# Memory values of layers two to four as Strassen's seven block products, in a one-core decoder trunk

## The chip, the cores and the metric

One core of a Trainium2 chip runs the whole kernel, in one launch. The metric is device time in microseconds from start to end of one execution; the median of three runs before the change is 2577.76 us. The engines are TensorE (PE in the profile, with its weight loads as PEld), VectorE (DVE), ScalarE (ACT), GpSimd (POOL) and SyncE (SP, which issues the weight loads).

## The reference

Four decoder layers over 256 tokens of width 2048. Each layer has self attention of one of three kinds, and four memory heads of size 256 that attend to 256 memory tokens. All four layers read the same normalized memory, each with its own weights:

```python
mem_n = _rmsnorm(mem, mem_norm)                 # (1, 256, 2048)
for i in range(DEPTH):                          # 4 layers
    h = _rmsnorm(x, norm_in[i])
    ...                                         # self attention, memory queries mq, gate
    mem_out = _memory_attention(mq, mem_n @ w_mem_kv[i])   # keys: columns 0..1023, values: 1024..2047
    y = jnp.concatenate([self_out, mem_out], axis=-1) * jax.nn.silu(gate)
    x = x + y @ w_out[i]
return _rmsnorm(x, final_norm)
```

The change concerns the second half of the columns of `mem_n @ w_mem_kv[i]`, the values, for i = 1, 2, 3. Everything is float32.

## The kernel before, in words

Products are made in float32r with each operand split in a high part and a low part, and three of the four partial products are kept. `split` (lines 60 and 69) makes the parts: ScalarE copies the source to the high part (`wh` from `wr`), VectorE subtracts it from the source for the low part (`wl`). Weights come by `stage`: SP loads 512 KB, four row blocks of 256 columns or two of 512, in a `wr` tile, of which there are five; `wh` and `wl` have three buffers each.

`memory()` runs ahead of the layers. It keeps the memory's features in `mT`, four tiles of four blocks of 128 features, high and low, 256 tokens. For each layer `i` and each half `p_` it does one values group and two keys groups:

- values: `rows_by(mT, 16, w, 0, (MEMW + p_ * 512, 512), "mv")`. For each of 16 feature blocks and each of two blocks of 128 tokens, three matmuls (lines 265 to 267) with the features as stationary weights and 512 weight columns streaming. `values()` scales the rows by `mrstd`, splits them and has GpSimd's queue store them (line 409).
- keys: `columns_by` (lines 285 and 289), twice with 256 columns, with the weights stationary and the features streaming, 512 wide for high and low features together and 256 wide for the low weights. `keys()` sums the two halves (`total`, line 296), multiplies by the token scales `mbc` (line 416), splits and has GpSimd's queue store them (line 418).

Each `stage` calls `other_work()`, which takes two steps of a queue of small jobs; `nm.first_chunk` (weighted parts of the first layer's input, line 198, and its square sums) is put there from the second half on. The layers then fetch keys and values back with GpSimd's queue. The instructions of an engine run in the order that a scheduler gave them when the program was built; GpSimd does almost no arithmetic: small copies that hold back table DMAs (`tick`, line 149), clearing, and eight casts of 128x256 (`xl`, line 827) in the sparse layer's selection. Behind the outputs of a layer, line 1146 adds a PSUM result to the residual `x`.

Of the kernel before, what the change touches and what calls it, by code (L numbers as in the profile page):

```python
# [2 lines left out]

# [28 lines left out]
def kernel(ctx: ExitStack, tc: tile.TileContext, a: dict, out: bass.AP,  # L32
# [10 lines left out]
    def misc(name, dt=F32):  # L43
        return ps.tile([P, 512], dt, name=name, tag="mp", bufs=4)

    def tmp(name, n=512, dt=F32):
        return wk.tile([P, n], dt, name=name, tag=f"t{n}", bufs=3)
# [5 lines left out]
    def f32(ap):  # L53
        return ap.bitcast(F32)

    def part_tile(dt=F32R):
        return wk.tile([P, 512], dt, name="hl", tag="hl", bufs=2)

    def copy_act(o, i, scale=1.0):
        inst = nc.scalar.activation(o, i, AF.Copy, scale=scale)  # L60
        if pinned:
            tc.keep_in_program_order(inst)
# [4 lines left out]
    def split(hi, lo, src):  # L67
        copy_act(hi, src)
        nc.vector.tensor_sub(lo, src, f32(hi))  # L69
# [58 lines left out]
    def bias_table(v):  # L128
        oh = wk.tile([32, N_TAB], F32, name="oh", tag="t512", bufs=3)
        tc.keep_in_program_order(nc.gpsimd.dma_start(oh, a["c_onehot"]))  # L130
        rb = wk.tile([32, 32], F32, name="rb", tag="rb", bufs=1)
        tc.keep_in_program_order(nc.gpsimd.dma_start(rb, a["rel_bias"]))
        mk = wk.tile([32, N_TAB], F32, name=f"mk{v}", tag="t512", bufs=3)
        tc.keep_in_program_order(nc.gpsimd.dma_start(mk, a["c_tabmask"][v]))
        pt = misc("pt")
        nc.tensor.matmul(pt[:32, :N_TAB], rb, oh, start=True, stop=True)
        tb = act.tile([P, 2, 4, S], F32, name=f"tb{v}", tag="y", bufs=2)[:32, 0, :2, :].rearrange(
            "p a b -> p (a b)")[:, :N_TAB]
        nc.vector.tensor_add(tb, pt[:32, :N_TAB], mk)
        nc.gpsimd.dma_start(flat[v], tb)  # L140
# [65 lines left out]
    def stage(w, k0, m, cols, each=None):  # L206

        n = cols[1] if len(cols) == 2 else cols[1] * cols[4]
        wr = wp.tile([P, ST * 512], F32, name="wr", tag="wr", bufs=WR)
        src = w[k0 * P:(k0 + m) * P, :].rearrange("(k p) n -> p k n", p=P)  # L210
        dst = wr[:, :m * n].rearrange("p (k n) -> p k n", k=m)
        if each is not None:
            for k in range(m):
                tc.keep_in_program_order(nc.sync.dma_start(dst[:, k, :], src[:, k, cols[0]:cols[0] + n]))
                each(k0 + k)
        elif len(cols) == 2:
            nc.sync.dma_start(dst, src[:, :, cols[0]:cols[0] + n])
        else:
            c0, r, step, off, width = cols
            for k in range(m):  # L220
                nc.sync.dma_start(dst[:, k, :].rearrange("p (r c) -> p r c", r=r),
                                  src[:, k, c0:c0 + r * step].rearrange("p (r c) -> p r c", r=r)
                                  [:, :, off:off + width])
        return wr, n
# [4 lines left out]
    def other_work():  # L229
        for _ in range(2):  # L230
            if steps and next(steps[0], None) is None:
                steps.pop(0)
# [34 lines left out]
                    nc.tensor.matmul(acc[t][:, :n], xl, wh[:, :n], start=False, stop=last)  # L267
        return acc

    def columns_by(xt, kts, w, k0, cols, name):  # L270

        acc = [ps.tile([P, 2, S], F32, name=f"acc_{name}{j}", tag="acc", bufs=4) for j in range(2)]
        for s in range(0, kts, 2 * ST):
            m = min(2 * ST, kts - s)
            wr, n = stage(w, k0 + s, m, cols)
            other_work()
            for k2 in range(0, m, 2):
                wh, wl = parts_of(wr, k2 * S, 2 * S)
                for k in range(2):
                    kt = s + k2 + k  # L280
                    q = xt[kt // 4]

                    for j in range(2):
                        o = k * S + j * P
                        nc.tensor.matmul(acc[j], wh[:, o:o + P], q[:, :, kt % 4, :],  # L285
                                         start=kt == 0, stop=False)
                    for j in range(2):
                        o = k * S + j * P
                        nc.tensor.matmul(acc[j][:, 0, :], wl[:, o:o + P], q[:, 0, kt % 4, :],  # L289
                                         start=False, stop=kt == kts - 1)  # L290
        return acc
# [73 lines left out]
    def memory():  # L365
        mrstd = cst.tile([P, 2], F32, name="mrstd")
        m16 = cst.tile([P, 2], F32, name="m16")
        mbc = act.tile([P, S], F32, name="mbc", tag="kr", bufs=1)
        mT = [act.tile([P, 2, 4, S], F32R, name="mT", tag=f"big{c}") for c in range(4)]
        mss = small("mss", 8, bufs=2)  # L370

        def each(k):

            if k % 2 and k < 15:
                mft[(k + 1) // 4].load((k + 1) // 2 % 2)
            if k == 15:
                tc.keep_in_program_order(nc.sync.dma_start(ident, a["c_ident"]))
                nc.vector.tensor_copy(identr, ident)

        def prepare(k):  # L380
            c = k // 4
            weighted_parts(mT[c], mft[c].q, k % 4, c * 4)

        def memory_rows(c):
            q = act.tile([P, 2, 512], F32, name="mrow", tag="pq", bufs=PQ)
            for t in range(2):
                tc.keep_in_program_order(
                    nc.sync.dma_start(q[:, t, :], min_[t][:, c * 512:(c + 1) * 512]))
            return q

        def row_scales(mrow):
            for c in range(4):
                for t in range(2):
                    square_sum(mss[:, t * 4 + c:t * 4 + c + 1], mrow[c][:, t, :])
            s2 = small("ms2", 2)
            nc.vector.tensor_reduce(s2, mss.rearrange("p (t c) -> p t c", t=2), AX.X, OP.add)
            rsqrt_mean(mrstd, s2, D)
            nc.vector.tensor_scalar(m16, mrstd, 0.0625, None, op0=OP.mult)
            spread(mbc, m16)

        def values(i, p_, acc):
            v = [act.tile([P, 2, 512], F32R, name="mv", tag="aux", bufs=AUX) for z in range(2)]
            for t in range(2):
                sc = mrstd[:, t:t + 1]
                copy_act(v[0][:, t, :], acc[t], scale=sc)
                nc.vector.scalar_tensor_tensor(v[1][:, t, :], acc[t], sc, f32(v[0])[:, t, :],
                                               op0=OP.mult, op1=OP.subtract)
            for z in range(2):
                nc.gpsimd.dma_start(mv[i][p_][:, z], v[z])

        def keys(i, h, acc):
            kT = act.tile([P, 2, 2, S], F32R, name="mkT", tag="pq", bufs=PQ)
            for j in range(2):
                z = total(acc[j])
                zs = wk.tile([P, S], F32, name="zs", tag="z", bufs=3)
                nc.vector.tensor_mul(zs, z, mbc)
                split(kT[:, 0, j, :], kT[:, 1, j, :], zs)
            nc.gpsimd.dma_start(mkT[i][h], kT)

        for i in range(depth):  # L420
            w = a["w_mem_kv"][i]
            for p_ in range(2):
                begins = i == p_ == 0
                if begins:

                    pinned.append(0)
                    acc = rows_by(mT, 16, w, 0, (MEMW, 512), "mv", prepare, each)
                    pinned.pop()
                    mrow = [memory_rows(c) for c in range(4)]
                else:  # L430
                    values(i, p_, rows_by(mT, 16, w, 0, (MEMW + p_ * 512, 512), "mv"))
                for h in (2 * p_, 2 * p_ + 1):
                    acck = columns_by(mT, 16, w, 0, (h * 256, 256), "mk")
                    if begins and h == 0:
                        row_scales(mrow)
                        values(i, p_, acc)
                    keys(i, h, acck)
                step = 2 * i + p_
                if begins:

                    not_before(f32(mT[3])[:, 0, 3, :1])
                    late_constants()
                    bias_table(0)
                    bias_table(1)
                if 1 <= step < 5:
                    steps.append(nm.first_chunk(step - 1))

# [57 lines left out]
    def spare(i, name, dt=F32):  # L505

        return wk.tile([P, 512], dt, name=name, tag=f"spare{i}", bufs=1)
# [725 lines left out]
```

## Time and profile before

| what | value |
|---|---|
| median of three runs | 2577.76 us (2576.88 to 2577.82) |
| profiled execution | 2576.9 us |
| its span, first to last instruction | 2575.1 us |
| granted TensorE clock | 0.999 |
| busy: PE, DVE, ACT, POOL | 2564.1, 1906.1, 1621.0, 87.1 us |
| memory stage, first value matmul of layer one to the last keys matmul of layer four | 5.9 to 363.3 us |

The memory stage consists of eight halves. A duration in the profile runs from an instruction's start to its modelled end, and instructions of one engine overlap a little; the distance between the starts of two neighbours in a busy row is what one costs there. A row of the table by stage has the stretch, its length, the busy time and number of instructions of each engine, the granted clock, the DMA engines' share and GB/s. A row of the timeline has start, length, engine, line, operation, output and inputs, and a count, with the idle time before it and its releaser in brackets. A row of the groups has the count, the busy time, the mean in ns, and the idle time ahead of them with its releasers.

### The profile page before, as it was taken

The page shows a single profiled execution, that of the slowest core. Times are in us where ns is not written, and L with a number is a line of the kernel's source. Part 1 is how long each engine was busy: PE and PEld are TensorE (multiplying, and loading weights), DVE is VectorE, ACT ScalarE, POOL GpSimd, SP SyncE. Part 2 cuts the span into 40 slices and gives each one's busy share as a digit, 9 for nine tenths or more (in the row PEclk, how much of TensorE's full clock was granted, in tenths as well). Part 3 has the DMA queues.
Part 4 walks back from the last instruction along what each step waited for, and adds up shares of the span by engine and source line. Part 5 has one row for each costly group of instructions (what it writes and reads, how often), then busy time and mean ns, then how long its engine had stood idle before and what let it go on. Part 6 is the DMA issues. An engine that isn't in the chain of part 4 may idle for free. (4 is left out here: it accounts for less than half of the span.)

```text
span 2575.1 us, 41628 instructions
## 1 busy us (share of the span) xinstructions
PE 2564.1 (100%) x13986; PEld 2208.4 (86%) x13986; DVE 1906.1 (74%) x4179; ACT 1621.0 (63%) x3467; POOL 87.1 (3%) x159
## 2 busy tenths in 40 slices
PE   9999999999999999999999999999999999999998
PEld 7888898888888888888888888888889888888887
DVE  6666667677777786887778776787878767777776
ACT  6556556556656566667666666676766655665665
POOL 1000000000000000000000000000000000000000
PEclk9999999999999999999999999999999999999999
DMA  9888777666676667566656575555655877676664
GB/s 303 258 259 267 239 212 235 185 170 191 196 201 201 203 213 246 173 197 188 196 165 197 170 226 170 169 183 185 196 156 148 241 201 198 196 196 181 212 173 179
DMA packets 459416, 520.02 MB, mean 202 GB/s; under 512 B 69520, under 2 KB 353056, under 8 KB 457536
## 3 DMA queue, kind: packets, MB, share of 16 engines
q1 hardware_dynamic: 441744, 449.72, 58.3%
q0 software_dynamic: 16736, 66.65, 8.0%
q8 instruction: 110, 1.80, 0.3%
q14 instruction: 106, 0.87, 0.1%
q10 hardware_dynamic: 720, 0.98, 0.1%
HBM read 494.10 MB, written 35.75 MB: 206 GB/s over the span
## 5 line engine op out<-in xcount | busy, mean ns | idle before, releaser
L69 DVE TENSOR_TENSOR wl<-wr,wh 128x512 fp32r<-128x512 f32 (+2 forms) x1720 | 1159.4, 677 | 579.1 <-ACT wh L60 555.5
L60 ACT ACTIVATE wh<-wr 128x512 fp32r<-128x512 f32 (+2 forms) x1720 | 1064.9, 621 | 801.7 <-PE acc_g L285 166.9
L285 PE MATMUL acc_g<-xT,wh 128*128 128x512 f32 x1536 | 484.7, 396 | 0.0
L289 PEld LDWEIGHTS acc_g<-xT,wl 128*128 128x128 f32 x1536 | 284.6, 188 | 63.0
L289 PE MATMUL acc_g<-xT,wl 128*128 128x256 f32 x1536 | 304.6, 280 | 0.0
L266 PE MATMUL acc_wo<-wl,y 128*128 128x512 f32 x752 | 297.3, 395 | 0.3 <-DVE wl L69 0.3
L267 PE MATMUL acc_wo<-wh,y 128*128 128x512 f32 x752 | 292.4, 390 | 0.0
L285 PEld LDWEIGHTS acc_g<-xT,wh 128*128 128x128 f32 x1536 | 235.9, 189 | 1.3
L265 PE MATMUL acc_wo<-wh,y 128*128 128x512 f32 x752 | 234.9, 392 | 0.1
L266 PEld LDWEIGHTS acc_wo<-wl,y 128*128 128x128 f32 x752 | 141.3, 188 | 28.5 <-DVE wl L69 1.2
L267 PEld LDWEIGHTS acc_wo<-wh,y 128*128 128x128 f32 x752 | 141.4, 188 | 27.1
L265 PEld LDWEIGHTS acc_wo<-wh,y 128*128 128x128 f32 x752 | 139.3, 188 | 28.5 <-ACT y L60 1.0
L285 PE MATMUL acc_mk<-mT,wh 128*128 128x512 f32 x512 | 161.5, 396 | 0.4 <-ACT wh L60 0.4
L285 PE MATMUL acc_mq<-xT,wh 128*128 128x512 f32 x512 | 161.6, 396 | 0.0
L1146 DVE TENSOR_TENSOR x<-x,acc_wo 128x512 f32<-128x512 f32 x184 | 122.3, 682 | 4.0 <-PE acc_wo L267 3.6
L285 PE MATMUL acc_qn<-cT,wh 128*128 128x512 f32 x384 | 121.3, 397 | 0.0
L285 PE MATMUL acc_cq<-xT,wh 128*128 128x512 f32 x384 | 120.9, 396 | 0.0
L289 PEld LDWEIGHTS acc_mk<-mT,wl 128*128 128x128 f32 x512 | 96.1, 188 | 22.8 <-DVE wl L69 0.4
L289 PEld LDWEIGHTS acc_mq<-xT,wl 128*128 128x128 f32 x512 | 93.7, 188 | 19.6
L289 PE MATMUL acc_mq<-xT,wl 128*128 128x256 f32 x512 | 103.4, 282 | 0.0
L266 PE MATMUL acc_q<-wl,xT 128*128 128x512 f32 x256 | 101.4, 396 | 0.0
L289 PE MATMUL acc_mk<-mT,wl 128*128 128x256 f32 x512 | 101.1, 278 | 0.0
(335 smaller groups left out, 4349.5 us busy)
## 6 DMA issues: line engine op xcount, KB each, us to landing
wr<-in_w_out_dram SPq DMA_DIRECT2D x188, 512.0 KB, 3.7
wr<-in_w_in_a_dram SPq DMA_DIRECT2D x176, 512.0 KB, 4.0
wr<-in_w_mem_kv_dram SPq DMA_DIRECT2D x120, 512.0 KB, 4.5
wr<-in_w_in_b_dram SPq DMA_DIRECT2D x112, 512.0 KB, 3.5
wr<-in_w_in_c_dram SPq DMA_DIRECT2D x104, 512.0 KB, 3.5
wr<-in_w_uq_dram SPq DMA_DIRECT2D x192, 128.0 KB, 2.9
wr<-in_w_uq_dram SPq DMA_DIRECT2D x48, 256.0 KB, 3.8
tab<-flat POOLq DMA_DIRECT2D x8, 1536.0 KB, 9.1
```

Source lines behind the costliest of these rows:

```text
L60: inst = nc.scalar.activation(o, i, AF.Copy, scale=scale)
L69: nc.vector.tensor_sub(lo, src, f32(hi))
L265: nc.tensor.matmul(acc[t][:, :n], xh, wh[:, :n], start=first, stop=False)
L266: nc.tensor.matmul(acc[t][:, :n], xh, wl[:, :n], start=False, stop=False)
L267: nc.tensor.matmul(acc[t][:, :n], xl, wh[:, :n], start=False, stop=last)
L285: nc.tensor.matmul(acc[j], wh[:, o:o + P], q[:, :, kt % 4, :], start=kt == 0, stop=False)
L289: nc.tensor.matmul(acc[j][:, 0, :], wl[:, o:o + P], q[:, 0, kt % 4, :], start=False, stop=kt == kts - 1)
L1146: nc.vector.tensor_add(xs, xs, acc[t])
```

## The change

For layers two to four (`if i:`) the values group becomes `seven(i, p_, w)`. The product of 256 tokens by 2048 features by 512 columns is cut in two along each side, and Strassen's seven products of 128 tokens by 1024 features by 256 columns take the place of the eight block products. Each is again three matmuls for each of its eight feature blocks, 256 columns wide, and all seven gather in four PSUM banks.

- The sums of features (`feature_sums`) are made once, as a job of the queue `steps` that starts after the first half of layer one: ten additions and multiplications of 128x1024 on GpSimd, six of 128x512 on VectorE, and their splits. They are kept in tiles that the layers use later.
- The sums of weights are made anew for each group: of a quarter's four weight blocks GpSimd (`add`, `sub`) makes five sums of 128x512 in `ws` tiles of three buffers, and seven sources are split, five sums and two plain blocks.
- A half has four such quarters (`j`). Behind each stands half of a keys group (`span`, eight of 16 feature blocks).
- `drain` scales the seven results on ScalarE, combines them on VectorE and GpSimd into the four blocks of the values, splits and stores them.

```diff
@@ -267,10 +268,12 @@
                     nc.tensor.matmul(acc[t][:, :n], xl, wh[:, :n], start=False, stop=last)
         return acc
 
-    def columns_by(xt, kts, w, k0, cols, name):
-
-        acc = [ps.tile([P, 2, S], F32, name=f"acc_{name}{j}", tag="acc", bufs=4) for j in range(2)]
-        for s in range(0, kts, 2 * ST):
+    def columns_by(xt, kts, w, k0, cols, name, acc=None, span=None):
+        if acc is None:
+            acc = [ps.tile([P, 2, S], F32, name=f"acc_{name}{j}", tag="acc", bufs=4) for j in range(2)]
+        for s in range(*(span or (0, kts)), 2 * ST):
             m = min(2 * ST, kts - s)
             wr, n = stage(w, k0 + s, m, cols)
             other_work()
@@ -417,9 +420,144 @@
                 split(kT[:, 0, j, :], kT[:, 1, j, :], zs)
             nc.gpsimd.dma_start(mkT[i][h], kT)
 
+        def homes():
+            def two(t):
+                q = t[:].rearrange("p a c -> p (a c)").rearrange("p (v k c) -> p v k c", v=2, k=4)
+                return [q[:, v] for v in range(2)]
+            def one(t):
+                return t[:, :512].rearrange("p (k c) -> p k c", k=4)
+            m1 = [two(act.tile([P, 4, S], F32R, name="as1", tag="gT", bufs=2)) for _ in range(2)]
+            m6 = [[one(part_tile()) for v in range(2)], [one(spare(z, "as6", F32R)) for z in range(2)]]
+            m7 = [[one(wk.tile([P, 768], F32R, name="as7", tag="pT", bufs=PT)) for v in range(2)]
+                  for _ in range(2)]
+            return {1: m1, 6: m6, 7: m7}
+        sums = {}
+        def feature_sums():
+            both = [act.tile([P, 2, 4, S], F32R, name="as25", tag="y", bufs=2) for c in range(2)]
+            sums.update(homes())
+            sums[2] = [[both[c][:, v, :, P:] for v in range(2)] for c in range(2)]
+            sums[5] = [[both[c][:, v, :, :P] for v in range(2)] for c in range(2)]
+            sums[3] = [[mT[c][:, v, :, :P] for v in range(2)] for c in range(2)]
+            sums[4] = [[mT[2 + c][:, v, :, P:] for v in range(2)] for c in range(2)]
+            for c in range(2):
+                f = []
+                for z in (c, c + 2):
+                    f.append(act.tile([P, 4, S], F32, name="fs", tag="pq", bufs=PQ))
+                    nc.gpsimd.tensor_add(f[-1], f32(mT[z])[:, 0], f32(mT[z])[:, 1])
+                    yield True
+                q = act.tile([P, 4, S], F32, name="fs", tag="pq", bufs=PQ)
+                nc.gpsimd.tensor_add(q, f[0], f[1])
+                yield True
+                split(both[c][:, 0], both[c][:, 1], q)
+                yield True
+                for z in f:
+                    nc.gpsimd.tensor_mul(z, z, mbc[:, None, :].to_broadcast([P, 4, S]))
+                    yield True
+                u, l = slice(0, P), slice(P, S)
+                for m, op, (x0, r0), (x1, r1) in ((1, nc.vector.tensor_add, (f[0], u), (f[1], l)),
+                                                  (6, nc.vector.tensor_sub, (f[0], l), (f[0], u)),
+                                                  (7, nc.vector.tensor_sub, (f[1], u), (f[1], l))):
+                    q = tmp("fm")[:].rearrange("p (k c) -> p k c", k=4)
+                    op(q, x0[:, :, r0], x1[:, :, r1])
+                    yield True
+                    split(sums[m][c][0], sums[m][c][1], q)
+                    yield True
+        def seven(i, p_, w):
+            bank = [misc(f"m7_{z}") for z in range(4)]
+            M = {3: bank[0][:, :S], 2: bank[0][:, S:], 5: bank[1][:, :S], 4: bank[1][:, S:],
+                 7: bank[2][:, :S], 6: bank[2][:, S:], 1: bank[3][:, :S]}
+            opened = {}
+            for j in range(4):
+                c = j // 2
+                b = []
+                for k0 in (2 * j, 8 + 2 * j):
+                    wr, _ = stage(w, k0, 2, (MEMW + p_ * 512, 512))
+                    other_work()
+                    q = wr[:, :1024].rearrange("p (k n c) -> p k n c", k=2, n=2)
+                    b += [q[:, :, 0, :], q[:, :, 1, :]]
+                add, sub = nc.gpsimd.tensor_add, nc.gpsimd.tensor_sub
+                for m, op, x0, x1 in ((2, None, 0, 0), (5, None, 3, 3), (1, add, 0, 3), (3, sub, 1, 3),
+                                      (4, sub, 2, 0), (6, add, 0, 1), (7, add, 2, 3)):
+                    q = b[x0]
+                    if op is not None:
+                        q = tmp("ws")[:].rearrange("p (k c) -> p k c", k=2)
+                        op(q, b[x0], b[x1])
+                    wh = wp.tile([P, 512], F32R, name="wh", tag="wh", bufs=3)
+                    wl = wp.tile([P, 512], F32R, name="wl", tag="wl", bufs=3)
+                    split(*(z[:].rearrange("p (k c) -> p k c", k=2) for z in (wh, wl)), q)
+                    for k in range(2):
+                        xh, xl = (z[:, j % 2 * 2 + k, :] for z in sums[m][c])
+                        cs = slice(k * S, (k + 1) * S)
+                        opens = j == k == 0 and m in (2, 5, 1, 6)
+                        if j == k == 0 and m in (3, 4, 7):
+                            with tc.issue_after(opened[{3: 2, 4: 5, 7: 6}[m]]):
+                                nc.tensor.matmul(M[m], xh, wh[:, cs], start=False, stop=False)
+                        else:
+                            inst = nc.tensor.matmul(M[m], xh, wh[:, cs], start=opens, stop=False)
+                            if opens:
+                                opened[m] = inst.ins
+                        nc.tensor.matmul(M[m], xh, wl[:, cs], start=False, stop=False)
+                        if (j, k) != (3, 1):
+                            nc.tensor.matmul(M[m], xl, wh[:, cs], start=False, stop=False)
+                        elif m in (2, 5, 6):
+                            opened[m] = nc.tensor.matmul(M[m], xl, wh[:, cs], start=False, stop=False).ins
+                        else:
+                            with contextlib.nullcontext() if m == 1 else                                     tc.issue_after(opened[{3: 2, 4: 5, 7: 6}[m]]):
+                                nc.tensor.matmul(M[m], xl, wh[:, cs], start=False, stop=True)
+                if j == 3:
+                    drain(i, p_, bank)
+                h = 2 * p_ + c
+                if j % 2 == 0:
+                    acc = columns_by(mT, 16, w, 0, (h * 256, 256), "mk", span=(0, 8))
+                else:
+                    columns_by(mT, 16, w, 0, (h * 256, 256), "mk", acc, (8, 16))
+                    keys(i, h, acc)
+        def drain(i, p_, bank):
+            s1, s2 = mrstd[:, 0:1], mrstd[:, 1:2]
+            xy = act.tile([P, 4, S], F32, name="vd", tag="pq", bufs=PQ)
+            wt = act.tile([P, 4, S], F32, name="vd", tag="pq", bufs=PQ)
+            for z in range(2):
+                copy_act(xy[:, 2 * z, :], bank[z][:, :S], scale=s1)
+                copy_act(xy[:, 2 * z + 1, :], bank[z][:, S:], scale=s2)
+            one = wk.tile([P, S], F32, name="vo", tag="z", bufs=3)
+            copy_act(one, bank[3][:, :S], scale=16.0)
+            nc.vector.tensor_add(wt[:, 0:2, :], xy[:, 0:2, :], xy[:, 2:4, :])
+            d = tmp("vd2")[:].rearrange("p (a c) -> p a c", a=2)
+            nc.gpsimd.tensor_sub(d[:, 0, :], xy[:, 3, :], xy[:, 2, :])
+            nc.gpsimd.tensor_sub(d[:, 1, :], xy[:, 0, :], xy[:, 1, :])
+            nc.vector.scalar_tensor_tensor(wt[:, 2:4, :], bank[2][:].rearrange("p (a c) -> p a c", a=2), 16.0,
+                                           one[:, None, :].to_broadcast([P, 2, S]), op0=OP.mult, op1=OP.add)
+            nc.vector.tensor_add(wt[:, 2:4, :], wt[:, 2:4, :], d)
+            v = [act.tile([P, 2, 512], F32R, name="mv", tag="aux", bufs=AUX) for z in range(2)]
+            q = [z[:].rearrange("p t c -> p (t c)").rearrange("p (a c) -> p a c", a=4) for z in v]
+            split(q[0][:, 1:3, :], q[1][:, 1:3, :], wt[:, 0:2, :])
+            split(q[0][:, 0::3, :], q[1][:, 0::3, :], wt[:, 2:4, :])
+            for z in range(2):
+                nc.gpsimd.dma_start(mv[i][p_][:, z], v[z])
         for i in range(depth):
             w = a["w_mem_kv"][i]
             for p_ in range(2):
+                if i:
+                    while not sums or steps and steps[0] is prep:
+                        other_work()
+                    seven(i, p_, w)
+                    if 1 <= 2 * i + p_ < 5:
+                        steps.append(nm.first_chunk(2 * i + p_ - 1))
+                    continue
                 begins = i == p_ == 0
                 if begins:
 
@@ -442,6 +580,8 @@
                     late_constants()
                     bias_table(0)
                     bias_table(1)
+                    prep = feature_sums()
+                    steps.append(prep)
                 if 1 <= step < 5:
                     steps.append(nm.first_chunk(step - 1))
```

1 line of the change is left out of this document (added).

## The prediction

> **What bounds the kernel now.** First the head of the page: the profiled execution took 2576.9 us, of which 2575.1 are its span; the median of the runs is 2577.76 (2576.88 to 2577.82). The sum below starts from 2576.9; that and the median differ by 0.03%.
>
> ```profile
> span 2575.1 us, 41628 instructions
> PE 2564.1 (100%) x13986; PEld 2208.4 (86%) x13986; DVE 1906.1 (74%) x4179; ACT 1621.0 (63%) x3467; POOL 87.1 (3%) x159
> PEclk9999999999999999999999999999999999999999
> ```
>
> TensorE is busy in the whole span at an undisturbed clock; GpSimd (POOL) does almost nothing. But the change sits in one stretch, so the next view is the table by stage: I cut the memory stage at the first value matmul of each half layer (a "half": one values group of 512 columns, two keys groups of 256).
>
> ```profile
> core 0: us, PE busy (x) PEld busy (x) DVE busy (x) ACT busy (x) POOL busy (x), PEclk, DMA share, GB/s
> 52.43:98.46 46.03, 46.03 (x230) 37.74 (x229) 28.32 (x49) 23.78 (x43) 8.84 (x17) 1.00 0.81 246
> 98.46:142.54 44.08, 44.08 (x227) 37.48 (x226) 28.81 (x50) 26.39 (x51) 2.13 (x4) 1.00 0.81 263
> 319.21:363.27 44.06, 44.06 (x227) 37.48 (x225) 26.84 (x46) 23.41 (x43) 2.13 (x4) 1.00 0.69 215
> 98.46:363.27 264.81, 264.81 (x1351) 225.29 (x1349) 171.93 (x310) 152.73 (x285) 12.75 (x24) 1.00 0.79 250
> ...
> DVE wl L69 <- ACT wh L60: 88.5, 144, 0.9
> ACT wh L60 <- PE acc_mk L285: 48.1, 66, 1.2
> ```
>
> The six halves of layers two to four fill 264.81 us, 44.1 each, and TensorE is never idle in them. The waits of that stretch (last two rows) say that VectorE waits for ScalarE's high part, and ScalarE for a buffer that TensorE still reads: both have room. VectorE has 44.1 - 28.8 = 15.3 us free per half. So TensorE time saved there would count in full, as long as VectorE's work and whatever hinders it stay under 44.1 us a half.
>
> **The change part by part.** TensorE first: what a 512 and a 256 wide matmul cost in sequence.
>
> ```profile
> L289 PE MATMUL acc_mk<-mT,wl 128*128 128x256 f32 x386 | 75.8, 278 | 0.0
> 473.52 0.88 PE L587 MATMUL msp<-mkr,mqT 128*128 128x256 f32 x6
> 121.41 0.39 PE L289 MATMUL acc_mk<-mT,wl 128*128 128x256 f32 x2
> 98.46:363.27 264.81, 131.61 (x576) 107.56 (x576) 8.43 (x12) 7.53 (x12) 1.00 0.79 250
> ```
>
> The last row is the value matmuls of the six halves: 576 of 512 columns fill 131.61 us, 0.228 each. One of 256 columns is shown as 0.28 from issue to end (first row), but six in a row take 0.88, so they are 0.12 apart, and two in 0.39 are 0.11 apart. Removed per half: 16 row blocks x 2 token blocks x 3 = 96 matmuls, 21.9 us. Added: 7 products x 8 row blocks x 3 = 168 of half the width, 168 x 0.12 = 20.2 us (18.8 at 0.112). TensorE saves 1.7 us a half, 10.2 in all (18.6 at most); I take 0.12, since those six change their weights each time as the products do. The keys' 22.2 us stay, cut in four pieces of 5.6 between four groups of products; the loads stay 16 of 512 KB a half and only change places in SP's queue, at a DMA share of 0.81 that a longer half lowers. If nothing else held, a half would take 42.4.
>
> Now the others. Per half:
>
> ```profile
> L69 DVE TENSOR_TENSOR wl<-wr,wh 128x512 fp32r<-128x512 f32 x190 | 130.9, 692 | 89.7 <-ACT wh L60 87.0 <-PE acc_mk L285 0.7
> L60 ACT ACTIVATE wh<-wr 128x512 fp32r<-128x512 f32 x190 | 119.4, 632 | 105.6 <-PE acc_mk L285 46.2 <-DVE wl L69 40.9 <-PE acc_mv L267 15.2
> L416 DVE TENSOR_TENSOR zs<-z,mbc 128x256 f32<-128x256 f32 x24 | 10.1, 422 | 0.4
> L406 DVE SCALAR_TENSOR_TENSOR mv<-acc_mv,mrstd,mv 128x512 fp32r<-128x512 f32 x12 | 8.4, 744 | 0.5 <-ACT mv L60 0.5
> L198 DVE SCALAR_TENSOR_TENSOR xT<-ft,gvec,xT 128x256 fp32r<-128x256 f32 x16 | 7.7, 479 | 0.0
> ...
> 943.15 0.68 DVE L69 TENSOR_TENSOR wl<-wr,wh 128x512 fp32r<-128x512 f32 x1
> 943.75 0.68 DVE L186 TENSOR_TENSOR xg<-tp,gvec 128x512 f32<-128x512 f32 x1
> 944.35 0.68 DVE L69 TENSOR_TENSOR xT<-xg,xT 128x512 fp32r<-128x512 f32 x1
> ```
>
> Weight splits go from 32 to 44 (28 for the products, 16 for keys). Back to back, a 512 wide VectorE operation starts every 0.60 us though shown as 0.68, so 0.08 of each duration overlaps. VectorE after the change: 44 splits, 2 adds and 2 splits of the drain, 48 x 0.605 = 29.0; one drain operation out of PSUM 0.67; 12 key operations x 0.34 (0.42 less the 0.08) = 4.1; the input features' parts 16 x 0.40 over six halves = 1.1. That is 34.9 us: alone it fits under 42.4. ScalarE has 46 x 0.63 = 29.0 for the same splits plus 5 drain copies and 8 of the keys of 256 columns, 13 x 0.4, 34 in all: it fits. The drain's chain itself ends in stores that nobody reads before layer two, so its place costs only the engines' time.
>
> GpSimd gets 20 adds of 128x512 a half and two of 128x256 in the drain. All the adds read SBUF twice, and the operation that fills VectorE (wl from wr and wh) reads SBUF twice as well. What happens when both run? This kernel has a few small GpSimd operations beside such splits:
>
> ```profile
> 395.43 0.18 POOL L149 COPY tick<-kr 128x1 f32<-128x1 f32 x1 [26.71 <-ACT kr L60]
> 583.87 0.68 DVE L69 TENSOR_TENSOR wl<-wr,wh 128x512 fp32r<-128x512 f32 x1
> 584.01 0.58 POOL L149 COPY tick<-x 128x1 f32<-128x1 f32 x1 [185.97 <-DVE x L1146]
> 958.27 0.40 POOL L827 CAST xl<-xT 128x256 fp32r<-128x256 f32 x1 [5.41 <-ACT xT L60]
> 958.33 0.89 DVE L69 TENSOR_TENSOR xT<-xg,xT 128x512 fp32r<-128x512 f32 x1
> 951.11 0.69 DVE L69 TENSOR_TENSOR xT<-xg,xT 128x512 fp32r<-128x512 f32 x1
> 951.14 1.72 POOL L827 CAST xl<-xT 128x256 fp32r<-128x256 f32 x2 [5.12 <-ACT xT L60]
> 951.72 0.89 DVE L69 TENSOR_TENSOR wl<-wr,wh 128x512 fp32r<-128x512 f32 x1
> 952.53 0.68 DVE L1146 TENSOR_TENSOR x<-x,acc_wo 128x512 f32<-128x512 f32 x1
> ```
>
> These rows carry the forecast. A copy of one element takes 0.18 alone and 0.58 when a split had started 0.14 us before it: it ended just after that split did. A 256 wide cast takes 0.40 alone; the split that started behind it took 0.89 in place of 0.68, 0.21 longer, which is the cast's length less the 0.19 of an empty operation. In the third case two casts meet two splits in a row: each cast lasts 0.86 and the second split 0.89. They take turns; the later one waits for the whole of the other's data. The last row's operand comes from PSUM, and it is not held.
>
> So each GpSimd add is a hold, H, that comes on top of VectorE's own time. How long is H for 512 columns with two inputs? No row shows such an add. The cast moves one input at (0.40 - 0.19) / 256 = 0.82 ns a column. One-input rate: H = 0.42. Two reads in turn: 0.84. Two reads and a write in turn: 1.26. The engine showed no faster rate, so 0.42 is the lower end; I take 1.05, midway between the two that count both reads. [...]
>
> VectorE and GpSimd together per half: 34.9 + 21 x 1.05 = 57.0. Of VectorE's time 3.1 us (operations with one SBUF input) could lie beside a hold, so 53.9 is the floor. Against 42.4 of TensorE this sum is the new bound: TensorE waits for its low parts.
>
> The chain is a little worse than the sum, because wh, wl and the sums (ws) have three buffers each. On both ScalarE and VectorE the built order of one quarter is five ws splits, four key splits, then two plain ones of the next group. The sums four and five and the first of the next quarter can begin only when a ws split has freed a buffer, so they fall between these splits: 6 x 0.605 + 4 x 1.05 = 7.8 us until the first key block is ready. Then TensorE takes 5.6 for the key blocks, during which VectorE has only three buffers to run ahead with; then 0.63 and a hand-over of 0.1 until the next ws split can start. A quarter is 14.1, four are 56.6; the keys' operations stand among the ws splits and add about 3.3, the drain's holds and adds 1.6: 61.5 a half. Between sum and chain I take 60, nearer the chain: 15.9 more than 44.1, six times, 95 us.
>
> The feature sums run once, from the end of the first half on: ten GpSimd operations of 1024 columns, 2.1 us of hold each, eight of them in the stretch 52.43 to 98.46, and on VectorE 12 operations of 0.605 and two of about 1.2. VectorE's 28.3 less 49 x 0.08 of overlap, + 9.7 + 16.8 = 50.9 against 46.0: +5, between 0 and +10. GpSimd's queue also issues the stores of keys and values; in the built order each stands ahead of adds of a later group, behind the operation that it waits for on VectorE by less than a quarter, and so costs little beside the holds.
>
> Sum: 2576.9 + 95 + 5 = 2677.
>
> **The rivals.**
> 1. Faster: the adds and the splits do not exclude each other, or the holds fall where VectorE waits. For it: 15.3 us are free per half. Against it: the three cases above, which are the same split. Then TensorE bounds it. The buffers just suffice: a released wh buffer needs 0.63 + 0.69 and hand-overs, 1.4, and two products on TensorE last 1.44. Time: 2576.9 - 10.2 = 2567 (2558 at 0.112). [...] It decides below H = (44.1 - 34.9) / 21 = 0.44.
> 2. Exclusion, but the add streams at the cast's rate, H = 0.42. The sum is 43.7, the chain 4 x (3.63 + 1.68 + 5.6 + 0.73) = 46.6, with the keys' operations 48: 2577 to 2604.
> 3. Dearer: GpSimd gets its turn only after two splits, not one, as long as VectorE has one ready. Against it stands the third case, where the cast came between two. Price: 4 x 0.6 in each quarter, 9.7 a half, 58 in all: 2736.
> That the products don't get cheaper is inside rival 1 (19 us at most) and would not be seen under the holds.
>
> **How the numbers follow.** The forecast has 0.82, each rival 0.06. With H = 0.84 and the bare sum a half takes 52.5: 2576.9 + 50 = 2627; with H = 1.26 and the chain, 65 and +10: 2712. For 8 in 10 I reach from rival 2's upper end to a little over the forecast's: 2605 to 2725. About 0.2%, 5 us, is what can be told from no change. Faster by more: rival 1, 0.06; within: the lower end of rival 2, 0.02; slower: the rest, 0.92.
>
> **What would show it.** In the profile after, halves of some 60 us in place of 44, TensorE idle in them for wl of line 70; wl from ws and from wr with a mean well over 0.69 us, up to 1.7; GpSimd adds of line 494 of 1.2 us alone and up to 1.8 behind a split; everything from the first layer's projections on unchanged in length. It would be wrong if wl stayed at 0.69 beside the adds, or if the halves came under 44 us.

## The result, and the profile after

The changed kernel takes 2725.03 us (median of four runs, 2723.87 to 2726.07) against 2577.79 before: a ratio of 1.0572, 95% interval 1.0554 to 1.059. It is slower, as forecast, and by more: 147 us where the forecast had 99.

The head of the page after, then the table by stage: from the second half of layer one to the first product, and the six halves of layers two to four.

```profile
span 2722.4 us, 42957 instructions
PE 2623.8 (96%) x14418; PEld 2251.9 (83%) x14418; DVE 2107.1 (77%) x4283; ACT 1678.4 (62%) x3577; POOL 312.3 (11%) x301
PE   9788878999999999999999999999999999999998
POOL 2555545200000000100000000000000000000000
PEclk9789998999999999999999999999999999999999
52.49:113.69 61.20, 48.79 (x224) 38.62 (x223) 48.52 (x57) 26.90 (x47) 31.33 (x24) 0.89 0.55 173
113.69:509.40 395.71, 320.53 (x1782) 266.51 (x1780) 349.42 (x407) 206.54 (x390) 209.87 (x157) 0.91 0.52 167
509.40:2722.40 2213.00, 2203.91 (x12171) 1904.72 (x12169) 1671.87 (x3744) 1408.87 (x3068) 64.82 (x113) 1.00 0.64 193
363.27:2575.10 2211.83, 2203.00 (x12166) 1903.81 (x12164) 1670.09 (x3742) 1408.52 (x3067) 63.58 (x111) 1.00 0.64 192
```

The last row is the kernel before, from its first layer's projections on: 2211.8 against 2213.0. So nearly the whole loss lies ahead of them: the six halves went from 264.8 to 395.7 (+130.9, 66.0 each in place of 44.1), the stretch with the feature sums from 46.0 to 61.2 (+15.2). TensorE is idle for part of both (busy 48.8 of 61.2 us and 320.5 of 395.7), and its granted clock is 0.89 and 0.91 there.

The groups and waits of the six halves:

```profile
L494 POOL TENSOR_TENSOR ws<-wr 128x512 f32<-128x512 f32 x120 | 180.9, 1519 | 157.4 <-DVE wl L70 111.9 <-DVE vd L543 18.2 <-DMA wr<-in_w_mem_kv_dram 15.8
L494 POOL TENSOR_TENSOR ws<-wr x120: 1259/1506/1829, 121.3 to 500.0; 128x512 f32<-128x512 f32 x120
L70 DVE TENSOR_TENSOR wl<-wr,wh 128x512 fp32r<-128x512 f32 x144 | 147.3, 1055 | 24.8 <-ACT wh L61 24.6
L70 DVE TENSOR_TENSOR wl<-ws,wh 128x512 fp32r<-128x512 f32 x120 | 138.5, 1173 | 15.8 <-ACT wh L61 13.9
L199 DVE SCALAR_TENSOR_TENSOR xT<-ft,gvec,xT 128x256 fp32r<-128x256 f32 x16 | 11.4, 732 | 0.0
ACT wh L61 <- PE acc_mk L288: 90.0, 79, 3.0
ACT wh L61 <- POOL ws L494: 16.9, 20, 2.4
PE m L510 <- DVE wl L70: 54.1, 69, 5.0
```

The second row gives the shortest, median and longest sum in ns. The same split that took 692 ns on average takes 1055 and 1173; TensorE waits 54 us for low parts in the products. A closer look, GpSimd's rows first, then VectorE's beside the last of them:

```profile
206.46 1.29 POOL L494 TENSOR_TENSOR ws<-wr 128x512 f32<-128x512 f32 x1 [4.18 <-DVE wl L70]
208.38 1.67 POOL L494 TENSOR_TENSOR ws<-wr 128x512 f32<-128x512 f32 x1 [0.63 <-DVE wl L70]
211.53 4.84 POOL L494 TENSOR_TENSOR ws<-wr 128x512 f32<-128x512 f32 x3 [1.49 <-DVE wl L70]
211.75 3.48 DVE L70 TENSOR_TENSOR wl<-wr,wh 128x512 fp32r<-128x512 f32 x2
215.15 1.50 DVE L199 SCALAR_TENSOR_TENSOR xT<-ft,gvec,xT 128x256 fp32r<-128x256 f32 x1
```

A sum alone takes 1.29, so by the prediction's reading of the casts (less the 0.19 of an empty operation; copies of one element that were not held took 0.18 to 0.20 in the kernel before) it holds for 1.10. Three sums in 4.84 and two splits in 3.48 take turns: one of each comes to 1.10 + 0.60 = 1.70. Here is the feature stretch:

```profile
62.57 0.51 POOL L133 DMA_DIRECT2D rb<-in_rel_bias_dram  x1
62.72 13.59 DVE L70 TENSOR_TENSOR wl<-wr,wh 128x512 fp32r<-128x512 f32 x2 [0.67 <-ACT wh L61]
63.59 2.40 POOL L457 TENSOR_TENSOR fs<-fs 128x1024 f32<-128x1024 f32 x1
65.94 4.62 POOL L454 TENSOR_TENSOR fs<-mT 128x1024 f32<-128x1024 f32 x2
70.53 4.63 POOL L462 TENSOR_TENSOR fs<-fs,mbc 128x1024 f32<-128x1024 f32 x2
75.76 0.80 PE L267 MATMUL acc_mv<-wl,mT 128*128 128x512 f32 x1 [10.57 <-DVE wl L70]
...
L70 DVE TENSOR_TENSOR wl<-wr,wh x32: 670/692/12984, 51.1 to 112.2; 128x512 fp32r<-128x512 f32 x32
```

There were no turns here: one split (the longest of the stretch, 12,984 ns, last row: shortest, median, longest) stood behind five GpSimd operations in a row, and TensorE 10.6 us behind the split. The first row is a DMA that GpSimd issues; the split began during it.

### The profile page after: what moved, and what is told of

Same layout as the page of the kernel before. It is cut to its first block, busy times and chain, and to the rows that moved or that the text cites. A ratio compares the mean times of both kernels' runs of the same rounds, so it can differ in the third digit from the quotient of the medians.

```text
span 2722.4 us, 42957 instructions
## 1 busy us (share of the span) xinstructions
PE 2623.8 (96%) x14418; PEld 2251.9 (83%) x14418; DVE 2107.1 (77%) x4283; ACT 1678.4 (62%) x3577; POOL 312.3 (11%) x301
## 3 DMA queue, kind: packets, MB, share of 16 engines
q1 hardware_dynamic: 441744, 449.72, 54.9%
## 5 line engine op out<-in xcount | busy, mean ns | idle before, releaser
L70 DVE TENSOR_TENSOR wl<-wr,wh 128x512 fp32r<-128x512 f32 (+3 forms) x1672 | 1190.6, 718 | 504.5 <-ACT wh L61 483.3
L61 ACT ACTIVATE wh<-wr 128x512 fp32r<-128x512 f32 (+3 forms) x1672 | 1034.2, 620 | 812.9 <-PE acc_g L288 168.6
L494 POOL TENSOR_TENSOR ws<-wr 128x512 f32<-128x512 f32 x120 | 180.9, 1519 | 157.4 <-DVE wl L70 111.9
L288 PE MATMUL acc_mk<-mT,wh 128*128 128x512 f32 x512 | 171.3, 417 | 0.8
L70 DVE TENSOR_TENSOR wl<-ws,wh 128x512 fp32r<-128x512 f32 x120 | 138.5, 1173 | 15.8 <-ACT wh L61 13.9
L292 PE MATMUL acc_mk<-mT,wl 128*128 128x256 f32 x512 | 109.4, 295 | 18.6 <-DVE wl L70 17.8
```

The source lines that it names most:

```text
L494: op(q, b[x0], b[x1])
```

## The experiments

Each run is one execution; the time of the kernel before on the same chip was 2576.8 to 2577.9, and the changed kernel's four runs lie within 2.2 us. e1, e2, e9 and e10 leave the sums out, so their values are not those of the reference. "Half" is the mean of the six halves of layers two to four, from the first product (or value matmul) to the first projection; "stretch" is what lies between the second half of layer one and them.

| run | edit | time, us | half | stretch |
|---|---|---|---|---|
| (changed kernel) | | 2725.0 | 66.0 | 61.2 |
| e1 | sums replaced by fills | 2624.8 | 49.0 | 61.0 |
| e2 | no sums | 2620.2 | 48.9 | 60.0 |
| e3 | sums on VectorE | 2691.5 | 60.6 | 59.7 |
| e5 | feature sums on VectorE | 2712.7 | 65.5 | 52.3 |
| e6 | keys in two pieces | 2706.2 | 62.9 | 59.8 |
| e7 | all sums on VectorE, two pieces | 2649.7 | 54.9 | 50.3 |
| e9 | no sums, two pieces | 2628.1 | 49.7 | 60.8 |
| e8 | TensorE kept busy | 2712.9 | 64.2 | 60.3 |
| e10 | no sums, four buffers of wh and wl | 2637.0 | 44.0 | 60.0 |
| e11 | four buffers | 2728.6 | 58.3 | 60.1 |
| e12 | before, 16 additions a half | 2607.7 | 49.2 | |
| e13 | before, 32 additions a half | 2751.7 | 72.5 | |
| e14 | shorter feature operations | 2716.4 | 66.4 | 51.0 |
| e15 | e7 with four buffers | 2701.7 | 56.5 | 44.9 |
| e16 | e6 with four buffers | 2739.2 | 60.5 | 59.9 |
| e17 | all sums on VectorE, four buffers | 2697.4 | 55.8 | 44.9 |

**Is it the exclusion, or that the sums come late?** Two theories: GpSimd's holds come on top of VectorE's time (theory 1); or GpSimd is only slow to deliver (theory 2). The first run fills the ws tiles with constants: GpSimd works nearly as long and still waits for a free tile, but it no longer reads SBUF. It also no longer waits for the loaded weights, for which the sums had stood 15.8 us in all six halves.

```diff
-                        op(q, b[x0], b[x1])
+                        nc.gpsimd.memset(q, 0.02)
+                        nc.gpsimd.memset(q, 0.03)
```

> Each of GpSimd's sums of weights is replaced by two fills of the same ws tile with a constant: GpSimd works nearly as long for each (2 x 0.58 us by the fills of 1152 columns in the trace, against 1.29 of a sum alone), the same waits and the same three buffers remain, but GpSimd no longer reads SBUF. Left out: the sums, so the values are meaningless. Theory 1 (a GpSimd operation that reads SBUF and a VectorE operation with two SBUF inputs exclude each other, so the holds come on top of VectorE's time): splits beside the fills go back to 0.69 us mean, the six halves to 43 to 46 us, the time to 2585 to 2605 (the 15 us of the feature sums stay). Theory 2 (the sums come late because of GpSimd's length and the three buffers, whatever it reads): halves stay above 60 us, time above 2690.

```profile
113.93:408.19 294.26, 279.80 (x1773) 244.01 (x1772) 229.44 (x405) 203.70 (x389) 147.04 (x277) 0.98 0.69 224
L494 POOL MEMSET ws<- 128x512 f32 x120 | 62.5, 524 | 127.5 <-DVE wl L70 110.1 <-DVE vd L544 6.9 <-ACT junk L204 6.3
L70 DVE TENSOR_TENSOR wl<-ws,wh 128x512 fp32r<-128x512 f32 x120 | 83.4, 696 | 32.2 <-ACT wh L61 30.3 <-PE m L518 1.0
```

GpSimd still works 2 x 0.52 us for each sum, and the splits are back at 696 ns; the halves fall by 17 us, 101 us in all. Lateness is too small for that: in the changed kernel ScalarE waited 16.9 us in all for sums (`wh` for `ws` in the rows above). So the reading is the main cost: theory 1. But the halves stand at 49.0, not at 43 to 46. The next run, without sums, says that this remainder has nothing to do with GpSimd's part in them:

```diff
-                    if op is not None:
-                        q = tmp("ws")[:].rearrange("p (k c) -> p k c", k=2)
-                        op(q, b[x0], b[x1])
```

> The sums of weights are left out: all seven products split plain weight blocks, GpSimd does nothing in a quarter. Left out: the sums, so the values are meaningless. Both theories: VectorE has 34.9 us a half and TensorE about 42.4, so halves of 42.4 to 44 and 2580 to 2595 with the feature sums' 15 us still in. This is the lower end for any way of making the sums. If the three buffers of wh and wl alone cost much (the rival of theory 1 in the quarter's chain), the halves would stay at 48 or more and the time at 2615 or more.

48.9: even with no sums to make, a half is longer than the 44.1 of before, with three buffers.

**The sums elsewhere.** Sums and drain subtractions on VectorE (e3), or only the feature operations (e5):

```diff
-                add, sub = nc.gpsimd.tensor_add, nc.gpsimd.tensor_sub
+                add, sub = nc.vector.tensor_add, nc.vector.tensor_sub
...
-                    nc.gpsimd.tensor_add(f[-1], f32(mT[z])[:, 0], f32(mT[z])[:, 1])
+                    nc.vector.tensor_add(f[-1], f32(mT[z])[:, 0], f32(mT[z])[:, 1])
```

> The sums of weights and the two subtractions of the drain are done by VectorE in place of GpSimd; the feature sums stay on GpSimd. Theory 1: each sum then costs VectorE 0.605 us in place of a hold of 1.1; VectorE has 34.9 + 20 x 0.605 + 0.7 = 47.7 us a half, more than TensorE's 42.4, so halves of 48 to 53 and 2616 to 2646: faster than the changed kernel, still slower than before. Theory 2 (only GpSimd's lateness): halves of 44 to 46, 2590 to 2605. If the work of VectorE did not matter at all, 2585.

> Only the ten one-time operations on features move from GpSimd to VectorE; the sums of weights stay on GpSimd. Theory 1, with GpSimd's operations back to back holding VectorE without a turn between them (one split stood 10.6 us behind five of them in the changed kernel): VectorE has 24.4 + 9.7 + 10 x 1.14 = 45.5 in a stretch of 46.0, so the stretch from the second half of layer one to the first product falls from 61.2 to 46 to 50 us and the time to 2710 to 2716. [...]

VectorE does the sums 5.4 us a half cheaper than GpSimd, as theory 1 has it in direction, but at 60.6 where its operations sum to 47.7 and I expected 48 to 53; neither theory's range was met. The feature operations on VectorE shorten the stretch by 8.9 us, to 52.3 where 46 to 50 was expected; the time came out as expected.

**The order, and the clock.** The keys' blocks in two pieces (e6; with everything on VectorE, e7; without sums, e9), and four idle matmuls ahead of the second matmul of 18 of a half's 28 products (e8):

```diff
+                    if m == 3:
+                        k1 = j % 2 * 8
+                        ...
+                        acc = columns_by(mT, 16, w, 0, (h * 256, 256), "mk", acc, (k1, k1 + 4))
```

```diff
+                        if k == 0 and j < 3 and (j > 0 or m in (3, 4, 6, 7)):
+                            for _ in range(4):
+                                ...
+                                    nc.tensor.matmul(bank[3][:, S:], xh, wh[:, cs], start=False, stop=False)
```

> As the changed kernel, but the keys' blocks of a quarter stand in two pieces of four blocks, one after the third product and one after the seventh, in place of one piece of eight behind the seven. Nothing else is changed; the work of each engine is the same. Theory A (what the changed kernel's 66 us a half have over the engine sum of VectorE and GpSimd holds, 58 us with the measured hold of 1.1, is that three buffers let VectorE run no further ahead than three splits, so that stretches of dear products and of cheap key blocks add up): halves of 59 to 62, 2685 to 2703. Theory B (the rest is something else, TensorE's lower clock or the late sums, that the order does not touch): halves of 64 to 67, 2713 to 2731.

> All sums (weights, features, drain) on VectorE, and the keys' blocks in two pieces as in the run before this one. GpSimd does no arithmetic. VectorE has 47.7 us a half by the sum of its operations; with the sums on VectorE and the keys in one piece the halves measured 60.6. Theory A: halves of 49 to 54, and 9 us less in the feature stretch: 2610 to 2640, the best form of the change, still slower than before. Theory B: halves of 58 to 61: 2667 to 2683.

> The sums of weights are left out (values meaningless) and the keys' blocks stand in two pieces. With one piece the halves measured 48.9, against 42.4 of TensorE's work. Theory A: halves of 43 to 45, 2583 to 2597. Theory B: 48 to 49, 2614 to 2621.

> The changed kernel with four more matmuls of 256 columns in front of the second matmul of most products, into a half bank that nobody reads: 9 to 10 us of TensorE work a half, put where it mostly waits for VectorE anyway. It tests what TensorE's granted clock, 0.91 over the six halves, costs. Theory C (the clock drops since TensorE stands idle, and the key blocks and products at half clock lengthen the path): clock above 0.97 in the halves, and they shorten by 2 to 5 us although work was added: 2695 to 2713. If the clock is only a symptom: the halves stay or grow by up to 5 us, 2725 to 2755, whatever the clock.

Spreading takes 3.1 us off a half, between the two theories' ranges, and with all sums on VectorE 5.7 (60.6 to 54.9, just over theory A's range; the time, 2649.7, between the two), which is the best form of the change; without sums it gains nothing (49.7, over both ranges), so the order was not what kept those halves at 49. With TensorE kept busy:

```profile
112.40:497.78 385.38, 341.85 (x2214) 296.63 (x2213) 342.60 (x407) 205.86 (x390) 213.32 (x157) 0.97 0.54 172
```

72 more matmuls a half, 8.6 us at 0.12, and the half is 1.7 us shorter, a little under the 2 to 5 expected: the clock went from 0.91 to 0.97. In the changed kernel it was 0.50 from 120 to 130 us, where TensorE was busy for 5.8 of the 10, and 1.00 from 135 to 160. That fits a clock that is a cost of its own, some 10 us of the 147. The added matmuls also shift when buffers come free, and no run separates the two.

**The buffers.** Four of wh and wl in place of three, without and with the sums; the space comes from one of four `aux` buffers:

```diff
-        wh = wp.tile([P, 512], F32R, name="wh", tag="wh", bufs=3)
+        wh = wp.tile([P, 512], F32R, name="wh", tag="wh", bufs=4)
```

> Sums of weights left out (values meaningless), and four buffers of wh and wl in place of three (the space is taken from one of four 'aux' buffers, which the drain uses two at a time; the later layers may lose a little by that, so the six halves are what is read). A product now frees a buffer after 0.72 us of TensorE, where the old value blocks took 1.36, while a copy and a split take 1.4 with hand-overs. Theory D (with three buffers that is just short, and every key or drain operation in between makes TensorE wait): halves fall from 48.9 to 43 to 45. Otherwise (the waits come from the work of ScalarE and VectorE as such) they stay at 48 or more.

> The changed kernel with four buffers of wh and wl in place of three, paid for in the same way. Theory 1 with the chain: halves fall from 66 towards the engine sum of VectorE and GpSimd's holds, 58: 60 to 64. If the late sums set the pace: 65 to 67.

```profile
113.15:377.12 263.97, 260.84 (x1774) 236.48 (x1772) 221.64 (x404) 198.25 (x390) 21.07 (x34) 1.00 0.78 249
112.26:462.18 349.92, 292.00 (x1766) 244.06 (x1764) 336.11 (x401) 200.39 (x388) 217.52 (x154) 0.97 0.60 188
```

The first row: TensorE busy for 260.8 of 264.0 us at full clock, 44.0 a half. The second: 58.3, under the range given, and the engine sum with the measured hold is 34.9 + 21 x 1.10 = 58.0. So three buffers cost 4.9 us a half without the sums and 7.6 with them (the clock is 0.97 here, so part may be the clock's). The times of these two runs are high since the later layers lose 46 and 52 us. I had put that down to the missing `aux` buffer, but e15 below keeps all four of those, gives up a load buffer instead, and loses 50 us in the later layers too, with the same waits (TensorE for ScalarE's `y`, seven times, 12.7 us in e11 and 12.4 in e15, none in the changed kernel). What these runs share is the fourth buffer of wh and wl, so the fourth buffer may carry that price itself; no run tried it alone.

**The reverse: GpSimd additions in the kernel before**, whose results nobody reads: one behind each load of layers two to four in e12, two in e13.

```diff
+        for _ in range(extra[0]):
+            nc.gpsimd.tensor_add(tmp("ws"), wr[:, :512], wr[:, 512:1024])
```

> The kernel before with one GpSimd addition of 128x512 behind each of the 16 weight loads of a half, in layers two to four; it reads the loaded block and writes a tile that nobody reads. Theory 1: VectorE has 25 us a half without its overlap and 16 x 1.1 = 17.6 of holds: 42.6, under TensorE's 44.1. So splits beside an addition last up to 1.8 us and their mean rises to 0.9 to 1.2, but the halves stay at 44 to 46 and the time at 2577 to 2590. If there is no exclusion in this arrangement, the mean stays at 0.69.

> As the run before this one, with two additions behind each load, 32 a half. Theory 1: 25 + 35 = 60 us of VectorE and holds a half, over TensorE's 44.1: halves of 60 to 66, 2672 to 2710, although nothing waits for GpSimd's results. No exclusion: 2577.

```profile
L69 DVE TENSOR_TENSOR wl<-wr,wh 128x512 fp32r<-128x512 f32 x190 | 180.0, 969 | 44.9 <-ACT wh L60 44.0
...
160.66 9.97 DVE L69 TENSOR_TENSOR wl<-wr,wh 128x512 fp32r<-128x512 f32 x4
160.90 0.57 POOL L421 DMA_DIRECT2D mkT<-mkT  x1 [2.78 <-DVE mkT L69]
161.49 7.39 POOL L225 TENSOR_TENSOR ws<-wr 128x512 f32<-128x512 f32 x6
169.49 0.80 PE L292 MATMUL acc_mk<-mT,wl 128*128 128x256 f32 x2 [6.11 <-DVE wl L69]
```

With 16 the splits rise to 969 ns as expected, but the halves grow by 5 us, to 49.2 where 44 to 46 was expected, although the sum, 42.6, is under TensorE's 44.1. I read this as delayed splits that three buffers don't make up; it was not tried with four. With 32 it is 72.5, over the range: the last four rows (of e13) show six additions without a turn for VectorE, as in the feature stretch.

**What was still open:** why there were no turns in the feature stretch (e14 halves the length of its operations), and what is left when both remedies are combined (e16) or VectorE does everything with enough buffers (e15, e17).

> The changed kernel with each one-time GpSimd operation on features cut in two of 512 columns; nothing else. In the changed kernel one split lasted 13.0 us while five such operations of 1024 columns ran one behind the other, though elsewhere splits and sums of 512 columns took turns. If the length of an operation decides whether VectorE gets its turn: no split over 3 us in the stretch from the second half to the first product, which falls from 61.2 to 50 to 55 us: 2714 to 2720. If it is that GpSimd's operations follow each other without waiting for another engine: the long split stays, 60 to 62 us, 2723 to 2728.

> All sums on VectorE, keys' blocks in two pieces, four buffers of wh and wl (paid for with one of the five buffers for loaded weights). VectorE's own sum is 47.7 us a half; with three buffers the halves measured 54.9. If the buffers are what is left: halves of 48 to 50, and with 6 to 8 us for the feature stretch 2605 to 2625, if four buffers for loaded weights do. If VectorE's order is: 53 to 55, 2638 to 2650.

> The changed kernel's sums on GpSimd, keys' blocks in two pieces and four buffers of wh and wl (paid for with one of four 'aux' buffers, so the later layers lose some 45 us as they did in the run with four buffers alone). Spreading gave 3.0 us a half with three buffers, the fourth buffer 7.6. If both work on the same thing (VectorE running ahead), the halves stay at the engine sum, 57 to 59. If the order is a cost of its own, 54 to 56.

> All sums on VectorE, keys' blocks in one piece as in the changed kernel, four buffers of wh and wl paid for with one 'aux' buffer (the later layers lose some 45 us, so the six halves are read). VectorE's own operations sum to 47.7 us a half, TensorE's to 42.4. With GpSimd's sums the same four buffers brought the halves to the engine sum, 58.3. If that holds here: halves of 47.5 to 50, so 20 to 35 us more than before in the six halves even where nothing holds VectorE. If VectorE's order or the chain costs more: 52 to 56.

In e14 turns were taken and the stretch fell to 51.0 (first row below: no split over 2.0 us). That looks like the length; but in e13 additions of the same 512 columns ran in rows without a turn, with one split of 13.5 us (second row). What decides it stays open. The traces have one thing in common, though. In the changed kernel about 100 weight splits stood behind one GpSimd operation and three behind more (12.98, 4.51 and 4.51 us); in e13 about 50 and 14. All these 17 began while GpSimd was issuing a DMA, or during the addition right behind such an issue; the rows at 62.57 and 160.90 above are two of the issues. It is not a full rule: the 2.01 us split of e14 began in one as well and let only one of two operations pass. No run moved the issues, so a cause is not shown.

```profile
L70 DVE TENSOR_TENSOR wl<-wr,wh x29: 673/693/2007, 51.1 to 96.2; 128x512 fp32r<-128x512 f32 x29
...
L69 DVE TENSOR_TENSOR wl<-wr,wh x193: 445/693/13477, 102.2 to 535.9; 128x512 fp32r<-128x512 f32 x191, 128x288 fp32r<-128x288 f32 x2
```

e16 gives 60.5, over both ranges and more than e11's 58.3: spreading helps with three buffers and hurts with four, so the agreement of e11 with the engine sum to 0.3 us is no law. e15 has 56.5, over both ranges too; it has one load buffer less, so its halves can't be set beside the others. e17 has 55.8, in the range for the order or the chain, against 47.7 of VectorE's operations. VectorE's sums stand in its own queue ahead of splits, and some wait there for loads (13.9 us in all in the six halves); whether that is the rest was not tried.

No form of the change came below the kernel before; the best took 2649.7.

## Why the prediction was right in its sign and wrong in its size

- The exclusion, the step that carried the forecast, held, and its size too: H was taken as 1.05, midway between two bounds, and comes to 1.10; sums took 1.26 to 1.83, as said. Without the reads, in e1, 101 us of the six halves went, the waits behind the holds and the clock (0.98) included.
- The price of TensorE's products held (their matmuls are 0.12 apart), but the saving never showed: without sums and with four buffers, TensorE nearly always busy, a half took 44.0. That is 1.6 over my 42.4 and no less than the 44.1 of before. Where the 1.6 went was not taken apart.
- **The step that failed is the chain, "between sum and chain I take 60".** 66.0 was measured, 36 of the 48 us missed. The chain had the three buffers in it, but at a full clock and with every hand-over on time, and I then went below its 61.5 because the engine sum was lower. With H at 1.10 the chain gives 4 x (3.63 + 4.40 + 5.6 + 0.73) + 4.9 = 62.3, so 3.7 us of a half lie outside it. (The 0.73 has the copy's 0.63 and 0.1 for the hand-overs, an estimate; in the kernel before, the copy at 200.40 us starts 0.04 behind the matmul that frees its buffer, the split 0.03 behind the copy.) The runs put the difference to the engine sum on the buffers: with a fourth 58.3, with three 66.0. The sum was a floor: of the runs with sums only e11 came near it, and e16 and e17 stayed 2.5 and 8.1 us above theirs with four buffers.
- TensorE's clock was not in the sum at all. It was 0.91 over the halves; e8, with TensorE kept busy, gets 1.7 us a half back. The other 2.0 outside the chain stay open, the two splits of 4.51 us among what may be in them.
- **The second term that was mis-sized is the feature stretch:** +5 forecast, +15.2 measured. I let sums and splits take turns there as well; five operations ran without a turn, and TensorE stood for 10.6 us. I had also said that GpSimd's DMA issues cost little beside the holds; this row began right behind one. Together 36 in the halves, 10 here and 1.2 in the later layers make 47 of the 48; the profiled run was 0.9 under the median.
- Rival 1 said that three buffers "just suffice" (1.4 against 1.44). They don't: without sums 48.9 with three, 44.0 with four. So its 2567 could not have come even without exclusion; e1, with the feature sums' 15 us still in it, took 2624.8.
- Rival 2's add at the cast's rate is out: a sum alone takes 1.26 to 1.29, where that rate gives 0.19 + 0.42. Rival 3's 2736 lies nearer to 2725 than my 2677, but by luck: a sum that let two splits pass would take 1.26 + 2 x 0.60 = 2.46, and the longest of the 120 took 1.83.
- One list was wrong: the input features' parts (line 199) read SBUF twice and are held as well, 479 ns before, 732 after.

## What to carry to other kernels

Before work is moved to GpSimd to spare VectorE, look in the trace for any GpSimd operation beside a VectorE operation with two SBUF inputs: if the later one is longer by the other's data time, as here (a split of 0.89 in place of 0.68 beside a cast of 0.40), the moved work takes that time from VectorE, here 1.10 us for an addition that VectorE does in 0.60. The sum of engine times was a floor here, not a forecast (58.0 against 66.0 with three buffers and 58.3 with four): where buffers just cover the copy and the split, as here (1.4 against 1.44), delays are passed on, so the chain's figure, and a lower clock (0.91 over the six halves here), belong in the number and the range. And a product that halves the matmul halves the time in which its buffers must be refilled, here from 1.36 to 0.72 us.

## What the runs showed of the hardware that I had not expected

GpSimd operations in a row sometimes let VectorE in between each two (a turn of 1.70 us) and sometimes not at all: one split stood for 13.0 us behind five operations of 1024 columns, another 13.5 us in the kernel before with added operations of 512. All the long waits of these two runs began during a DMA issue of GpSimd or the operation right behind it, which is not shown to be the cause. It went the other way as well: at 106.12 us of the changed kernel, right behind such an issue, a GpSimd multiplication of 1024 columns took 9.00 us, 2.33 elsewhere, while eleven VectorE operations ran one behind the other. TensorE's granted clock was 0.86 over the six halves of the kernel before with 32 additions (e13), where TensorE was busy for 309.5 of 434.9 us, and 0.91 in the changed kernel, where TensorE was busy 81% of the time (320.5 of 395.7 us).
